# The opening of a hybrid attention and GLA layer: inputs laid out by the host, sums of squares by products with ones, and first groups of one K tile

## The chip, the core and the metric

The kernel runs on one NeuronCore of a Trainium2 chip. TensorE (PE) multiplies matrices from SBUF into PSUM; VectorE (DVE) and ScalarE (ACT) do the elementwise work; GpSimd (POOL) here does little but start transfers; SyncE (SP) starts nearly all the loads of weights. Each engine runs its own list of instructions in the order of the built program and waits on semaphores for the others. The metric is the device time of one execution in microseconds (us): the median of the runs, and, for where the time goes, one profiled execution.

## What is computed

One layer (batch 1, 256 latent tokens, 256 context tokens, width 2048, everything in float32). Only the latent stream is returned. The part that the change touches is the beginning: the modulation and the first columns of the input projection.

```python
def rms_norm(x, g):
    xf = x.astype(jnp.float32)
    y = xf * lax.rsqrt(jnp.mean(xf * xf, axis=-1, keepdims=True) + EPS)
    return (y * g.astype(jnp.float32)).astype(x.dtype)

def modulate(x, g, shift, scale):
    return rms_norm(x, g) * (1 + scale) + shift
...
mod_x = jnp.split((jax.nn.silu(c) @ w_mod[l] + b_mod[l])[:, None, :], 6, axis=-1)
mod_c = jnp.split((jax.nn.silu(c_ctx) @ w_mod[l] + b_mod[l])[None, None, :], 6, axis=-1)
...
qa, ka, va, qb, kb, vb, rb, gf, gb, gate_a, gate_b = proj(modulate(x, g_mix[l], mod_x[0], mod_x[1]))
...
cqa, cka, cva, cqb, ckb, cvb, crb, cgf, cgb, cgate_a, cgate_b = proj(modulate(ctx, g_mix[l], mod_c[0], mod_c[1]))
```

`h @ w_in` is cut into the inputs of two token mixers: windowed attention (qa, ka, va) and gated linear attention, GLA (qb, kb, vb, rb, and a low-rank decay). Their outputs are merged by sigmoid gates and projected; then comes a convolutional feed-forward part with `w_up` and `w_down`.

## The kernel before

The stream h = modulate(x) is kept transposed, with the 2048 channels on partitions in 16 K tiles of 128, and 256 tokens in the free dimension; s = 0 is the latent stream, s = 1 the context. Every float32 operand of the large products is split into a high part (`hi`, rounded to the fast float32 format) and a remainder (`lo`), and a product is three fast products: hi.hi, lo.hi and hi.lo. Weights arrive as `raw` [128, 2, 512] (two K tiles of 512 columns, 512 KB); `wsplit_raw` (lines 223 to 236) makes `whi` on ScalarE (L227) and `wlo` on VectorE (L228). The products themselves all go through `mm` (L83).

**The opening** (lines 114 to 660) needs shift and scale of a K tile before that K tile of h exists. `mod_both` (from line 329) computes both streams' modulation for a group of K tiles: `mraw` loads of 1 MB from `w_mod`, small products with SiLU(c) and SiLU(c_ctx) in `cS` into four quarters of a PSUM bank (`pm`, L95), a transposition on VectorE (`mtr`, L347), a product with `sel` that adds the quarters (`pcol`), four copies and the bias (L357, L360). A group of n K tiles takes n loads for the scale (part 1) and n for the shift (part 0). The groups are `[(0, 2), (2, 2), (4, 4), (8, 4), (12, 4)]` (line 449): first K tile and number.

For each group the kernel computes four blocks of columns of the projection over the group's K tiles and adds them up in SBUF: `qb` (two blocks of 512 columns, latent only), `kbt` (512 columns of K, both streams) and `vb0` (512 columns of V, both streams). That is done in this order so that the first products can start before all of `w_mod` has arrived. `affine_scale` (L528, L531) multiplies by the scale and the row factor, `affine_shift` (L538, L539) adds the shift and splits into hi and lo.

**Tokens before.** x and ctx are loaded as rows of tokens; TensorE transposes them in 128x128 pieces (`turn_tokens`, L481), ScalarE and VectorE copy the pieces into `xr`. The squares are summed per token (`square`, L472, L473), `rms_scale` makes a factor per token on [128, 2], and a product of ones with a diagonal matrix spreads it to a row for all partitions (`factor_row`, L503). The parameters c, b_mod, g_mix and the like are loaded as rows and turned by TensorE (`columns`).

**Order of work.** Inside the opening `pe_seq` chains all of TensorE's instructions in the order of the program text, and `load` chains the loads on SP's queue. VectorE's and ScalarE's lists are ordered by a scheduler at build time; `hold`, `hold_hi` and `in_order` place a few instructions by hand. `idle(n)` puts n transposes of the identity on TensorE. `bg_steps` holds the modulation steps of the next group, which `tick` issues between blocks at `bg_rate`. The tiles named M share 16 buffers of 8 KB per partition (line 37): xr, kbt, vb0, the h tiles, mraw and others; `raw` has 7, `whi` and `wlo` 3 each, the PSUM banks `acc` 4.

After the opening come the low-rank decay products (`plr`, L695, its first consumer of the whole of h), GLA, attention, merge and the feed-forward part. TensorE works through these one after the other.

Of the kernel before, what the change touches and what calls it, by code (L numbers as in the profile page):

```python
# [8 lines left out]
F32 = mybir.dt.float32  # L9
# [7 lines left out]
P = 128  # L17
D = 2048
# [12 lines left out]
def layer_kernel(ctx, tc, A, out):  # L31
# [81 lines left out]

    ident = cst.tile([P, P], F32, name="ident")
    load(ident, A["k_ident"])
    x00 = M("x00", [P, D])
    load(x00, A["x"][0][0:P, :])
    crow = sm.tile([32, P], F32, name="crow", tag="t128", bufs=2)
    nc.scalar.dma_start(crow[0:16, :], A["c"][0].rearrange("(k p) -> k p", p=P))
    nc.scalar.dma_start(crow[16:32, :], A["c_ctx"].rearrange("(k p) -> k p", p=P))  # L120
    sel = cst.tile([P, 34], F32, name="sel")
    G.dma_start(sel, A["k_sel"])
    ones = cst.tile([P, P], F32, name="ones")
    V.memset(ones, 1.0)

    silu_c = S.activation(crow, crow, AF.Silu)
    with tc.issue_after(silu_c.ins):
        S.preload_act_table_set("natural_log_exp_and_others")
    cS = W2("fb", "cS", [P, KT, 32])
    V.memset(cS, 0.0)  # L130
    ccol = cst.tile([P, KT], F32, name="ccol")
    pt = bank("pc0", (P, 32))
    PE.transpose(pt, crow, ident[:32, :32])
    for i in range(2):
        V.tensor_copy(cS[:, :, i], pt[:, 16 * i:16 * i + 16])
    V.tensor_copy(ccol, pt[:, 0:16])

    def columns(name, parts, eng=G, put=None):
        rows = sm.tile([P, P], F32, name="rows", tag="t128", bufs=2)
        n = 0  # L140
        for ap in parts:
            k = ap.shape[0] // P
            eng.dma_start(rows[n:n + k, :], ap.rearrange("(k p) -> k p", p=P))
            n += k
        t = cst.tile([P, n], F32, name=name)

        def turn():
            pt = bank("pt_" + name, (P, P))
            turn_b(pt[:, :n], rows[:n, :], ident[:n, :n])
            V.tensor_copy(t, pt[:, :n])  # L150

        if put is None:
            turn()
        else:
            put(turn)
        return t

    turn_c1 = []
    c1 = columns("c1", [A["b_mod"][0], A["g_mix"][0], A["g_ffn"][0]], put=turn_c1.append)
    bmod, gmix, gffn = c1[:, 0:96], c1[:, 96:112], c1[:, 112:128]  # L160
# [168 lines left out]
    def mod_both(part, t0, n, dst, put=None):  # L329


        a = []
        c0, w = part * D + t0 * P, n * P
        nk = 16 // n

        def step(k0):
            if k0 == 0:
                a.append(bank(f"pm{part}_{t0}", (P, w), side=True))
            raw = M("mraw", [P, nk, w])
            load(raw, w_mod[k0 * P:(k0 + nk) * P, c0:c0 + w].rearrange("(c p) d -> p c d", p=P))  # L340
            for k in range(nk):
                kt = k0 + k
                q = 32 * (kt % 4)
                mm_b(a[0][q:q + 32, :], cS[:, kt, :], raw[:, k, :], start=(kt < 4), stop=(kt >= 12))
            if k0 == KT - nk:
                tr = W2("fb", "mtr", [P, n, 4, 32])
                V.transpose(tr.rearrange("p a b c -> p (a b c)"), a[0])  # L347
                a.append(tr)
                if put is not None:
                    put(end)  # L350

        def end():
            pc = bank(f"pcol{part}_{t0}", (32, n * 4, 2))
# [4 lines left out]
            b0 = part * 16 + t0  # L358
            d = dst[:, :, t0:t0 + n]
            V.tensor_tensor(d, d, bmod[:, b0:b0 + n].unsqueeze(1).to_broadcast([P, 2, n]), op=ALU.add)  # L360

        steps = [lambda k0=k0: step(k0) for k0 in range(0, KT, nk)]
# [71 lines left out]
    def rms_scale(ss, n, shape):  # L434
# [14 lines left out]
    groups = [(0, 2), (2, 2), (4, 4), (8, 4), (12, 4)]  # L449
    mods = [[mod_both(part, t0, n, dst, put) for part, dst in ((1, scale1), (0, shift1))]  # L450
            for (t0, n), put in zip(groups, [None, None] + 3 * [lambda fn: defer(0, fn)])]

    xr = [M(f"xr{i}", [P, 8, T]) for i in range(4)]
# [4 lines left out]
    def load_tokens(s):  # L458
        x = []
        for t in range(2):  # L460
            x_ = x00
            if s or t:
                x_ = M(f"x{s}{t}", [P, D])
                load(x_, A["ctx" if s else "x"][0][t * P:(t + 1) * P, :])
            x.append(x_)
        return x

    def square(eng, x_, t, ss):

        junk = (kbt, vb0)[t].rearrange("p a b -> p (a b)")  # L470
        if eng is S:
            return S.activation(junk, x_, AF.Square, accum_out=ss[:, t:t + 1]).ins  # L472
        return V.scalar_tensor_tensor(junk, x_, 1.0, x_, op0=ALU.mult, op1=ALU.mult,  # L473
                                      accum_out=ss[:, t:t + 1]).ins

    def turn_tokens(s, t, x_):
        for g in range(4):
            pt = bank("ptx", (P, 4, P), side=True)
            for k in range(4):
                kt = g * 4 + k  # L480
                i = PE.transpose(pt[:, k, :], x_[:, kt * P:(kt + 1) * P], ident)  # L481
                if not s + t + kt:
                    opening[:] = [i.ins]
                pe_seq(i)
            dst = xr[2 * s + g // 2][:, (g % 2) * 4:(g % 2) * 4 + 4, t * P:(t + 1) * P]
            if g % 2:
                i = V.tensor_copy(dst, pt).ins
            else:
                S.activation(dst, pt, AF.Copy)
        return i  # L490

    def factors(ss):
        cols = rms_scale(ss, D, [P, 2])
        dgs = [sm.tile([P, P], F32, name="dg", tag="t128", bufs=2) for _ in range(2)]
        for t in range(2):
            V.tensor_scalar(dgs[t], ident, cols[:, t:t + 1], None, op0=ALU.mult)
        return dgs

    def factor_row(s, dgs):

        pr = bank("pr", (P, T), side=True)
        for t in range(2):
            pe_seq(PE.matmul(pr[:, t * P:(t + 1) * P], ones[:, 0:P], dgs[t], start=True, stop=True))  # L503
        r = W2("fa", f"rrow{s}", [P, T])
        S.activation(r, pr, AF.Copy)
        rrow1.append(r)
# [19 lines left out]
    def affine_scale(s, t0, n):  # L526
        sc = scale1[:, s, t0:t0 + n]
        V.scalar_tensor_tensor(sc, sc, 1.0, gmix[:, t0:t0 + n], op0=ALU.add, op1=ALU.mult)  # L528
# [34 lines left out]


    x_t = load_tokens(0)
    sums = [sm.tile([P, 2], F32, name="ss0", tag="ss0", bufs=2) for _ in range(2)]
    square(S, x_t[0], 0, sums[0])
    i = turn_tokens(0, 0, x_t[0])
    in_order(i, square(V, x_t[1], 1, sums[0]))
    turn_tokens(0, 1, x_t[1])  # L570
    turn_c1[0]()
    (a0, a1, ea), (b0, b1, eb) = mods[0]
    a0()
    dgs = factors(sums[0])
    a1()
    factor_row(0, dgs)
    idle(8)
# [3 lines left out]
    idle(12)  # L581
    b1()
    idle(6)
    eb()
    idle(14)
    more_h(0)
    qb0 = [W2("fc", "qb0", [P, 512]) for _ in range(4)]
    kts = ALL[0:2]
    early.extend(wload(w_in[0:2 * P, QB + j * 512:QB + j * 512 + 512]) for j in range(2))
    x_t = load_tokens(1)  # L590
    raws = [wload(w_in[0:2 * P, c:c + 512]) for c in (KB, VB)]
# [3 lines left out]
    proj_T(w_in, QB, kts, [h_all(0)], add_to(lambda i: qb0[i], True))  # L595
    sq0 = square(S, x_t[0], 0, sums[1])
    sq1 = square(V, x_t[1], 1, sums[1])
    proj_T(w_in, QB + 512, kts, [h_all(0)], add_to(lambda i: qb0[2 + i], True))
    in_order(last_lo[0], sq1)
    hold_hi.append(sq0)  # L600
    hold.append(sq1)
    early.append(wsplit_raw(raws[0]))
    dgs = factors(sums[1])
    for t in range(2):
        turn_tokens(1, t, x_t[t])
    early.append(wsplit_raw(raws[1]))
    (a0, a1, ea), (b0, b1, eb) = mods[1]
    a0()
    factor_row(1, dgs)
    a1()  # L610
    affine_scale(1, *groups[0])
    affine_shift(1, *groups[0])

    def mid_k():
        ea()
        b0()
        for s in range(2):
            affine_scale(s, *groups[1])

    def mid_v():  # L620
        eb()
        hi.append(affine_shift(0, *groups[1])[1])

    def evac_v(i, b):
        if i < 2:
            V.tensor_copy(vb0[:, i, :], b)
        else:
            in_order(hi[0], S.activation(vb0[:, i, :], b, AF.Copy).ins)

    hi = []  # L630
    proj_T(w_in, KB, kts, [h_all(0), h_all(1)], add_to(lambda i: kbt[:, i, :], True), mid=mid_k)
    b1()
    early.extend(wload(w_in[2 * P:4 * P, c:c + 512]) for c in (QB, QB + 512, KB, VB))
    proj_nat(w_in, 0, VB, kts, h_xc, evac_v, mid=mid_v)
    affine_shift(1, *groups[1])

    for gi, (t0, n) in enumerate(groups):
        if gi == 0:
            continue
# [5 lines left out]
        if gi + 1 < len(groups):  # L645
            bg_steps.extend(mods[gi + 1][0] + mods[gi + 1][1])
            ticks = 4 * ((n + 1) // 2)
            bg_rate[:] = [(1.4 if gi > 1 else 1.0) * len(bg_steps) / ticks + 0.01, 0.0]
        if t0 == 8:
            more_h(1)  # L650
        for s in range(2):
            if gi > 1:
                affine_scale(s, t0, n)
                affine_shift(s, t0, n)
# [4 lines left out]
        proj_nat(w_in, 0, VB, kts, h_xc, add_to(lambda i: vb0[:, i, :], False), mid=flush if gi == 1 else None)  # L659
# [649 lines left out]
```

## Time and profile before

| | us |
|---|---|
| median of 3 runs | 2007.79 (2007.24 to 2007.80) |
| span of the profiled execution, first to last instruction | 2005.1 |
| first product with `w_in` (L83) | starts 27.87 |
| first decay product (L695), after the opening | starts 209.29 |

The page gives no time of its own for the profiled execution beside its span; the median lies 2.7 us above the span. In a time line each row has the start, the length, the engine, the line, the operation, output and inputs with their shape, the count where several are merged, and in brackets the idle time of the engine before it and what ended that. A float32 product that isn't in the fast format appears as two records for one instruction. A row of waits gives who waited for whom, the total, the number of times and the longest.

### The profile page before, as it was taken

The numbers are of one execution on the slowest core, as the hardware profiler recorded it, in microseconds if no ns is written. First come the engines' busy times: TensorE is split into PE (matmuls) and PEld (weight loads), VectorE is DVE, ScalarE is ACT, GpSimd is POOL, SyncE is SP. The second block draws the span as 40 slices with busy tenths as digits, with TensorE's granted clock in tenths as the row PEclk, the third lists the DMA queues.
The fourth block names the chain that finished last, engine by engine and source line by source line (L and its number), as shares of the span: only waits on it lengthen the run. The fifth ranks groups of instructions, "written<-read, shape, count | busy, mean of one in ns | idle before, by whom it ended". The sixth has DMA issues, their size and how long they took to land.

```text
span 2005.1 us, 27521 instructions
## 1 busy us (share of the span) xinstructions
PE 1977.6 (99%) x10450; PEld 1645.9 (82%) x10450; DVE 1435.7 (72%) x2241; ACT 960.5 (48%) x1395; POOL 45.0 (2%) x66
## 2 busy tenths in 40 slices
PE   7999999999999999999999999999999999999999
PEld 5679888888877777888888888888888888888887
DVE  5666667877858888978876455898887555667754
ACT  4323464562345655444444444655555334555532
POOL 1000010011000000000000000000000000000000
PEclk9999999999999999999999999999999999999999
DMA  9986222326754456888886665587876656666563
GB/s 338 386 295 187 86 84 74 104 78 215 222 171 114 126 173 197 286 287 289 286 283 230 233 208 189 170 292 255 257 240 218 215 191 190 189 189 189 190 213 113
DMA packets 214149, 413.56 MB, mean 206 GB/s; under 512 B 12420, under 2 KB 20884, under 8 KB 212992
## 3 DMA queue, kind: packets, MB, share of 16 engines
q1 hardware_dynamic: 212464, 406.96, 63.4%
q0 software_dynamic: 1488, 4.82, 0.8%
q8 instruction: 82, 1.34, 0.3%
q14 instruction: 51, 0.42, 0.1%
q10 hardware_dynamic: 64, 0.02, 0.0%
HBM read 409.63 MB, written 2.11 MB: 205 GB/s over the span
## 4 chain that ended last, share of the span: by engine, by line
PE 60%; issue 16%; DVE 0%; POOL 0%; ACT 0%; DMA 0%; DVEq 0%; POOLq 0%
PE acc L83 47%; PE accs L83 12%; PE pto L98 0%; POOL att L913 0%; DMA glan<-in_gla_norm 0%; PE ptx L98 0%; POOL att L911 0%; PE pcl L95 0%; DVE yd L1252 0%; DVE yd L1246 0%; ACT yo L1128 0%; ACT whi L227 0%; ACT x1T L1136 0%; DVE og L1059 0%; DVE dg L1169 0%
## 5 line engine op out<-in xcount | busy, mean ns | idle before, releaser
L227 ACT ACTIVATE whi<-raw 128x1024 fp32r<-128x1024 f32 x568 | 601.5, 1059 | 814.6 <-PE acc L83 635.4
L228 DVE TENSOR_TENSOR wlo<-raw,whi 128x1024 fp32r<-128x1024 f32 x568 | 693.8, 1223 | 406.3 <-ACT whi L227 345.8
L391 DVE SCALAR_TENSOR_TENSOR macc<-raw,ccol,macc 128x512 f32<-128x512 f32 x240 | 179.8, 749 | 3.8
L83 PE MATMUL acc<-h,whi 128*128 128x512 f32 x704 | 176.9, 393 | 0.6 <-DVE h L523 0.6
L83 PE MATMUL accs<-h,whi 128*128 128x512 f32 x704 | 176.3, 392 | 0.0
L83 PEld LDWEIGHTS acc<-h,whi 128*128 128x128 f32 x704 | 126.5, 189 | 23.7 <-DVE h L523 0.9
L83 PEld LDWEIGHTS accs<-h,whi 128*128 128x128 f32 x704 | 126.6, 189 | 22.6
L83 PE MATMUL acc<-whi,h00hi 128*128 128x512 f32 x352 | 140.4, 399 | 1.0 <-DVE val L62 0.5
L83 PE MATMUL acc<-whi,h01hi 128*128 128x512 f32 x352 | 140.2, 398 | 0.0
L83 PE MATMUL acc<-whi,h00lo 128*128 128x512 f32 x352 | 138.4, 393 | 0.0
L83 PE MATMUL acc<-whi,h01lo 128*128 128x512 f32 x352 | 138.0, 392 | 0.0
L83 PE MATMUL acc<-whi,al 128*128 128x512 f32 x352 | 137.1, 389 | 0.0
L83 PE MATMUL acc<-whi,ah 128*128 128x512 f32 x352 | 137.0, 389 | 0.0
L83 PEld LDWEIGHTS acc<-h,wlo 128*128 128x128 f32 x704 | 96.2, 190 | 7.0
L83 PEld LDWEIGHTS accs<-h,wlo 128*128 128x128 f32 x704 | 96.0, 190 | 6.9
L83 PE MATMUL acc<-wlo,h01hi 128*128 128x512 f32 x352 | 98.6, 395 | 0.0
L83 PE MATMUL acc<-h,wlo 128*128 128x256 f32 x704 | 98.3, 282 | 0.0
L83 PE MATMUL accs<-h,wlo 128*128 128x256 f32 x704 | 98.2, 282 | 0.0
L83 PE MATMUL acc<-wlo,h00hi 128*128 128x512 f32 x352 | 97.8, 394 | 0.0
L83 PE MATMUL acc<-wlo,ah 128*128 128x512 f32 x352 | 94.5, 389 | 0.0
L83 PEld LDWEIGHTS acc<-whi,h00hi 128*128 128x128 f32 x352 | 66.4, 189 | 16.5 <-DVE val L62 1.0
L83 PEld LDWEIGHTS acc<-whi,ah 128*128 128x128 f32 x352 | 66.1, 188 | 13.6
(393 smaller groups left out, 3473.3 us busy)
## 6 DMA issues: line engine op xcount, KB each, us to landing
raw<-in_w_in SPq DMA_DIRECT2D x208, 512.0 KB, 4.5
raw<-in_w_up SPq DMA_DIRECT2D x176, 512.0 KB, 4.3
raw<-in_w_mod SPq DMA_DIRECT2D x128, 512.0 KB, 4.5
raw<-in_w_down SPq DMA_DIRECT2D x88, 512.0 KB, 3.7
mraw<-in_w_mod SPq DMA_DIRECT2D x32, 1024.0 KB, 13.4
raw<-in_w_attn_o SPq DMA_DIRECT2D x32, 512.0 KB, 4.9
raw<-in_w_gla_o SPq DMA_DIRECT2D x32, 512.0 KB, 5.1
raw<-in_w_out SPq DMA_DIRECT2D x32, 512.0 KB, 3.7
```

Source lines behind the costliest of these rows:

```text
L83: r = pe_seq(PE.matmul(*a, **k))
L227: j = S.activation(hi[:, 0:n, :], raw[:, 0:n, :], AF.Copy).ins
L228: i = V.tensor_tensor(lo[:, 0:n, :], raw[:, 0:n, :], hi[:, 0:n, :].bitcast(F32), op=ALU.subtract).ins
L391: i0 = V.scalar_tensor_tensor(a[0], raw[:, k, :], ccol[:, kt:kt + 1], a[0], op0=ALU.mult, op1=ALU.add).ins
```

## The change

- The host lays out x and ctx transposed by K tiles (`xT`, `ctxT`), c and c_ctx as columns (`k_c`), the parameters as columns (`k_cols1`, `k_cols2`), and the shift and scale columns of `w_mod` by group and load (`w_mod01`), so that a load of 1 MB is 8 KB in a row on each partition.
- The transposes of tokens and parameters, the sums per token and the diagonal matrices go. The latent stream's squares are summed over channels by 16 products with ones into `pr`; the context's squares are added up on VectorE first and take one product. The row factor is then computed on a full [128, 256] row, on all partitions alike. The Newton step's factor -0.5 moves into `gm1`.
- The groups become `[(0, 1), (1, 1), (2, 2), (4, 4), (8, 4), (12, 4)]`. The first two have one K tile each, with one load per modulation part, a plain copy in place of the transposition, and their own loads of weights (`wrow`: one K tile of 1024 columns of qb, or 512 of K beside 512 of V) and products (`row_T`, `row_nat`).
- The order of the first two groups: latent K tile 0; modulation of K tile 1 with its column products; the context's product with ones; latent qb of K tile 1; the context's K and V of K tile 0; modulation of the next group between the K and V products of K tile 1.
- The four column turns of conv_w, conv_b and the gate biases become one load of `cw`. The background rate for the first group of two K tiles is set by hand.

```diff
+    def load_tokens(s):
+        for i in range(4):
+            k = slice((i % 2) * 4, (i % 2) * 4 + 4)
+            load(xr[2 * s + i // 2][:, k, :], A["ctxT" if s else "xT"][i // 2, :, k, :])
...
-    silu_c = S.activation(crow, crow, AF.Silu)
+    silu_c = S.activation(cS[:, :, 0:2], crow, AF.Silu)
...
+    V.tensor_scalar(gm1, gmix, -0.5, None, op0=ALU.mult)
...
-            load(raw, w_mod[k0 * P:(k0 + nk) * P, c0:c0 + w].rearrange("(c p) d -> p c d", p=P))
+            load(raw, A["w_mod01"][part, t0 + i].rearrange("p (c d) -> p c d", c=nk))
...
+                if n == 1:
+                    tr = W2("fb", "mtr", [P, P])
+                    V.tensor_copy(tr, a[0])
...
+            if n == 1:
+                pc = bank(f"pcol{part}_{t0}", (P, 2, 1))
+                mm_b(pc[:, :, 0], a[1], sel[:, 0:2], start=True, stop=True)
+                V.tensor_tensor(d, pc, bias, op=ALU.add)
+                return
...
-    groups = [(0, 2), (2, 2), (4, 4), (8, 4), (12, 4)]
+    groups = [(0, 1), (1, 1), (2, 2), (4, 4), (8, 4), (12, 4)]
...
+    def square_sums(s, dst):
+
+        pr = bank("pr", (P, T), side=True)
+        for i in range(4):
+            x_, o = (t[:, (i % 2) * 4:(i % 2) * 4 + 4, :] for t in (xr[2 * s + i // 2], dst[i // 2]))
+            if i % 2:
+                V.tensor_tensor(o, x_, x_, op=ALU.mult)
             else:
+                S.activation(o, x_, AF.Square)
+            if s == 0:
+                for k in range(4):
+                    pe_seq(PE.matmul(pr, ones[:, 0:P], o[:, k, :], start=(i + k == 0), stop=(i + k == 6)))
+        if s:
+            a, b = dst
+            V.tensor_tensor(a, a, b, op=ALU.add)
+            for n in (4, 2, 1):
+                V.tensor_tensor(a[:, 0:n, :], a[:, 0:n, :], a[:, n:2 * n, :], op=ALU.add)
+        return pr
+
+    def factor_row(pr):
+
+        r = W2("fa", "rrow", [P, T])
+        u = W2("fa", "vrow", [P, 2, T])
+        v, t = u[:, 0, :], u[:, 1, :]
+        V.tensor_scalar(v, pr, 1.0 / D, EPS, op0=ALU.mult, op1=ALU.add)
+        S.activation(r, v, AF.Ln)
+        S.activation(r, r, AF.Exp, scale=-0.5)
+        V.tensor_tensor(t, r, r, op=ALU.mult)
+        V.tensor_tensor(t, t, v, op=ALU.mult)
+        V.scalar_tensor_tensor(r, t, -3.0, r, op0=ALU.add, op1=ALU.mult)
...
+    def wrow(kt, c0, step):
+
+        raw = wr.tile([P, 2, 512], F32, name="raw", tag="raw")
+        load(raw, w_in[kt * P:(kt + 1) * P, c0:c0 + 2 * step].rearrange("p (b c) -> p b c", b=2)[:, :, 0:512])
+        return raw
...
+    opening[:] = [pe_seq(PE.transpose(warm[:, 0:P], ident, ident)).ins]
+    idle(16)
+    pr = square_sums(0, [t.rearrange("p a b -> p (a b)").rearrange("p (a b) -> p a b", a=8) for t in (kbt, vb0)])
+    idle(6)
+    (a0, ea), (b0, eb) = mods[0]
     a0()
+    factor_row(pr)
+    idle(6)
     ea()
     b0()
     affine_scale(0, *groups[0])
+    idle(10)
     more_h(0)
     qb0 = [W2("fc", "qb0", [P, 512]) for _ in range(4)]
+    raws = [wrow(0, QB, 512), wrow(0, KB, 1024)]
+    eb()
+    idle(6)
     i, j = affine_shift(0, *groups[0])
     hold.append(i)
     hold_hi.extend([None, j])
+    wq = wsplit_raw(raws[0])
+    load_tokens(1)
+    wkv = wsplit_raw(raws[1])
+    row_T(0, wq, (0, 1), [h_all(0)], add_to(lambda i: qb0[i], True))
+    row_T(0, wkv, (0,), [h_all(0)],
+          lambda i, b: V.tensor_copy(kbt[:, 2 * i:2 * i + 2, 0:T], b.rearrange("p (f t) -> p f t", f=2)))
+    row_nat(0, wkv, h_x, lambda i, b: S.activation(vb0[:, i, :], b, AF.Copy))
+    (a0, ea), (b0, eb) = mods[1]
     a0()
+    b0()
+    raws = [wrow(1, QB, 512), wrow(1, KB, 1024)]
+    ea()
+    eb()
+    affine_scale(0, *groups[1])
+    i, j = affine_shift(0, *groups[1])
+    hold.append(i)
+    hold_hi.append(j)
+    sq = [M(f"sq{i}", [P, 8, T]) for i in range(2)]
+    pr = square_sums(1, sq)
+    pe_seq(PE.matmul(pr, ones[:, 0:P], sq[0][:, 0, :], start=True, stop=True))
+    wq = wsplit_raw(raws[0])
+    row_T(1, wq, (0, 1), [h_all(0)], add_to(lambda i: qb0[i], False))
+    factor_row(pr)
+    for g in (0, 1):
+        affine_scale(1, *groups[g])
+        affine_shift(1, *groups[g])
+    wkv1 = wsplit_raw(raws[1])
+    row_T(0, wkv, (0,), [h_all(1)],
+          lambda i, b: V.tensor_copy(kbt[:, 2 * i:2 * i + 2, T:2 * T], b.rearrange("p (f t) -> p f t", f=2)))
+    row_nat(0, wkv, [h_tok(1, 0), h_tok(1, 1)], lambda i, b: S.activation(vb0[:, 2 + i, :], b, AF.Copy))
+    for fn in mods[2][0]:
+        fn()
+    row_T(1, wkv1, (0,), [h_all(0), h_all(1)], add_to(lambda i: kbt[:, i, :], False))
+    for fn in mods[2][1]:
+        fn()
     early.extend(wload(w_in[2 * P:4 * P, c:c + 512]) for c in (QB, QB + 512, KB, VB))
+    row_nat(1, wkv1, h_xc, add_to(lambda i: vb0[:, i, :], False))
...
-            bg_rate[:] = [(1.4 if gi > 1 else 1.0) * len(bg_steps) / ticks + 0.01, 0.0]
+            bg_rate[:] = [1.4 * len(bg_steps) / ticks + 0.01, 0.0] if gi > 2 else [1.3, -2.0]
...
+    cw = cst.tile([P, 368], F32, name="cw")
+    G.dma_start(cw, A["k_cols2"])
```

231 lines of the change are left out of this document (75 added, 156 removed).

## The prediction, made before the result was seen

> **What bounds the kernel now.** I read the head of the page first, then the busy time by stage, then the time line of the opening engine by engine, because every edited line but a few belongs to the first 209 us.
>
> ```profile
> span 2005.1 us, 27521 instructions
> PE 1977.6 (99%) x10450; PEld 1645.9 (82%) x10450; DVE 1435.7 (72%) x2241; ACT 960.5 (48%) x1395; POOL 45.0 (2%) x66
> PE 60%; issue 16%; DVE 0%; POOL 0%; ACT 0%; DMA 0%; DVEq 0%; POOLq 0%
> ...
> 14.50:17.50 3.00, 1.07 (x16) 0.50 (x16) 1.96 (x9) 0.41 (x2) 0.00 (x0) 1.00 1.09 349
> 17.50:21.20 3.70, 3.45 (x23) 2.19 (x24) 0.45 (x1) 0.33 (x1) 0.00 (x0) 0.54 1.09 350
> 24.00:27.80 3.80, 3.80 (x42) 2.85 (x40) 1.39 (x7) 1.55 (x3) 0.00 (x0) 1.00 1.05 417
> 34.20:43.40 9.20, 7.65 (x73) 5.08 (x71) 7.03 (x17) 5.93 (x13) 1.05 (x3) 1.00 1.09 348
> 43.40:84.90 41.50, 41.02 (x303) 28.99 (x302) 27.20 (x65) 11.63 (x21) 1.03 (x2) 1.00 1.05 382
> 84.90:209.20 124.30, 123.15 (x877) 103.02 (x873) 77.83 (x136) 39.09 (x52) 7.52 (x12) 1.00 0.75 247
> ```
>
> The window rows give stretch, length, busy time of PE, PEld, DVE, ACT and POOL, granted clock, DMA share and GB/s. TensorE is busy to 99% and is the only engine with a share in the chain of waits, so a microsecond in which TensorE has no product ready is a microsecond of time. In the opening the DMA share is also full (1.05 to 1.09), yet from 43.4 on TensorE is busy in 41.02 of 41.5 us: the feed keeps pace. The median of the runs, 2007.8, is 2.7 us over the span; I sum against the span and add 2.7.
>
> ```profile
> 7.04 3.87 PE L481 MATMUL ptx<-ident,x 128*128 128x128 f32 x16
> 24.35 1.07 PE L95 MATMUL pm<-mraw,cS 128*32 128x256 f32 x16
> 27.87 0.39 PE L83 MATMUL acc<-h00hi,whi 128*128 128x256 f32 x1
> 33.33 1.12 PE L83 MATMUL acc<-h00hi,wlo 128*128 128x256 f32 x8
> 34.29 1.47 PE L481 MATMUL ptx<-ident,x 128*128 128x128 f32 x12
> 40.30 1.07 PE L95 MATMUL pm<-mraw,cS 128*32 128x256 f32 x16 [0.25 <-ACT xr L489]
> 74.76 2.48 DVE L548 TENSOR_TENSOR kb<-kb,acc 128x512 f32<-128x512 f32 x4 [1.78 <-PE acc L83]
> 81.97 1.19 PE L83 MATMUL acc<-wlo,h00hi 128*128 128x512 f32 x4
> 209.29 0.64 PE L695 MATMUL plr<-h00hi,wlr 128*32 128x256 f32 x8
> ```
>
> Products with w_in run without a break from 27.87 to the decay products at 209.29. Eight 128x256 products follow each other in some 0.96 us, 0.12 each; four 128x512 ones in 1.03, 0.26 each. One modulation load (16 records) costs TensorE 1.07. VectorE adds 128x512 from the accumulators in 0.62 (four in 2.48).
>
> **The start.** The change loads x already turned, so x's 32 transposes go, and forms the sum of squares by sixteen full float32 products with ones.
>
> ```profile
> 6.77 1.28 ACT L128 ACT_TABLE_LOAD   x1
> 11.56 2.28 DVE L473 SCALAR_TENSOR_TENSOR vb<-x 128x2048 f32<-128x2048 f32 x1
> 14.97 0.28 DVE L150 COPY c<-pt_c 128x128 f32<-128x128 f32 x1
> 20.87 0.38 ACT L505 ACTIVATE rrow<-pr 128x256 f32<-128x256 f32 x1 [5.07 <-PE pr L503]
> 22.80 0.17 DVE L360 TENSOR_TENSOR scale<-scale,c 128x4 f32<-128x4 f32 x1
> 22.89 1.53 PE L562 MATMUL warm<-ident 128*128 128x128 f32 x12
> 23.00 0.23 DVE L528 SCALAR_TENSOR_TENSOR scale<-scale,c 128x2 f32<-128x2 f32 x2
> 23.29 0.88 DVE L531 SCALAR_TENSOR_TENSOR xr<-xr,scale,rrow 128x256 f32<-128x256 f32 x2
> 25.49 0.45 DVE L347 STREAM_TRANSPOSE mtr<-pm 128x256 f32<-128x256 f32 x1 [1.32 <-PE pm L95]
> 27.31 0.91 ACT L538 ACTIVATE h00hi<-xr,shift 128x256 fp32r<-128x256 f32 x2 [1.15 <-DVE shift L360]
> 269.01 1.03 PE L95 MATMUL pa<-q,kf 128*128 128x256 f32 x4
> 269.88 1.03 PE L95 MATMUL pa<-q,kg 128*128 128x256 f32 x4
> ```
>
> The price of such a product: two (four records) start 0.87 us after the two before, so 0.43 each, sixteen 6.9. Seventeen warm-up transposes at the cold rate (3.87 for 16), from some 4.4 us, when I take the identity to have landed, end at about 8.5; ScalarE's first square is ready by then, since its second table load ends by 8.05 as now. So the sums end near 15.4. Behind them come six small steps on DVE and ACT (0.38 to 0.48 each with hand-over) and the 0.28 copy, 3.0 in all; the scale's bias, factor and first multiplication, 0.9: 19.3. The shift's products, its copy, ten warm-ups, column product and bias run beside that and end at 20.9; hi takes 0.5 and the first product starts near 21.7 instead of 27.87: **-6.2**. Bounds: with the sums at the full clock from the start and loads as early as now, 20.5; with a cold clock for half the sums (8 x 0.43 more), 25.
>
> **Context tokens.** Their 32 transposes and what waits on them fill TensorE from 34.29 to 40.30: **-6.0**. In their place stands one product with ones (0.43), counted in the next wait. Against this, only two modulation loads instead of four lie ahead of the first product, so two more lie behind it, and a load for one K tile needs 32 records of half the width: 2 x 1.07, and between nothing and 0.5 more for each of the two narrow ones behind it (sixteen weight loads take 0.50 in the row from 14.5 to 17.5): **+2.5**.
>
> **What opens in between.** With one K tile, little work is ready. The built program's order on VectorE, which runs it in that order, shows three places where TensorE stands.
>
> First: x's part of K tile 0 is 36 products of 256 and 6 of 512 columns, 5.7 us, to about 27.9; the two loads of K tile 1 last to 30.7. Their column products need two copies of the sums, but VectorE has ahead of the first copy: two evacuations of K (0.62 each), two squares of the context (1.2 each) and the addition of 128x2048 (2.28), which waits for ScalarE's two squares, themselves behind the evacuation of V. That addition ends near 33.3. Then copy, additions of 1024 and 512, second copy, two biases, an addition of 256, factor, multiplication: 3.7; hi and the conversion of the next weights on ScalarE, 1.5 (0.46 and the 1.06 of whi): product at 38.5. From 30.7 that is 7.8, less 0.6 for the three small products in it: **+7.2**. Behind the blocked column product stand all of TensorE's later instructions.
>
> ```profile
> L227 ACT ACTIVATE whi<-raw 128x1024 fp32r<-128x1024 f32 x568 | 601.5, 1059 | 814.6 <-PE acc L83 635.4
> L228 DVE TENSOR_TENSOR wlo<-raw,whi 128x1024 fp32r<-128x1024 f32 x568 | 693.8, 1223 | 406.3 <-ACT whi L227 345.8
> ```
>
> Second: the 24 query products end at 41.4, but the context's factor row stands on VectorE behind two wlo (2.4) and four additions to qb (4 x 0.62): 38.5 + 2.4 + 2.5 = 43.4, then three steps of the factor, a multiplication and hi, 2.3: 45.7. **+4.3**.
>
> Third: in the first group of two K tiles the second lo stands on VectorE behind wlo, the first lo, four additions to vb and two more wlo. From the shift's column product: copies and bias 0.82, 3 x 1.2, 4 x 0.62, two lo 0.9, together 7.8; TensorE has 12 products of 512 and three of 256 columns for it, 3.4. **+4.4**. Twice, too, a column product follows its loads with nothing between them, so it waits out the transposition (0.45 and hand-overs): **+2.0**. At the group of four K tiles five loads and both column products stand together ahead of the first product, and lo waits for copies, factor, four multiplications and one wlo (4.4 against 1.5 of work, and 1.5 for the second column product, less the 0.8 below): **+3.5**.
>
> Now there are waits there as well, which go with the old order:
>
> ```profile
> PEld pm L95 <- DMA mraw<-in_w_mod: 2.1, 3, 1.1
> ...
> PEld acc L83 <- ACT h10hi L538: 1.1, 2, 0.8
> PEld acc L83 <- ACT h00hi L538: 0.8, 1, 0.8
> ...
> PEld acc L83 <- DVE h10lo L539: 0.3, 1, 0.3
> ```
>
> 2.1, 1.1 and 0.3: **-3.5** (the 0.8 is used above). Bounds of the five waits together (21.4): half, if the steps on VectorE overlap better than added up, and a quarter more, 27, if each hand-over costs 0.1.
>
> **The clock.** In 14.5 to 17.5 TensorE was busy for 1.07 of 3.0 us, and in the next 3.7 us the granted clock was 0.54. Waits of 7.2, 4.3 and 4.4 us leave such stretches; each costs half of some 3.5 us, 1.75. Bounds 0 and 5.3 (all three); I take two: **+3.5**. "TensorE: Matmul & The Clock Gate" of the Trainium skill (Part 1) says that a window of about 3.4 us must be idle before the clock is halved. By that rule only the first wait is sure to hold one, and the sum would be 1.75 less, 2017.8; the row shows the fall after a window that was a third busy.
>
> Hidden or nothing: the column turns of conv_w and its like (three or four products of under 0.3) go, a gain under 1. The loads laid out for the host's order change no byte count. Past the opening the engines' orders differ in a few neighbouring steps only, which I cost at nothing.
>
> **Sum.** -6.2 - 6.0 + 2.5 + 7.2 + 4.3 + 4.4 + 2.0 + 3.5 - 3.5 + 3.5 = +11.7. Span 2016.8, time **2019.5**.
>
> **The rivals.** *The feed sets the pace (faster).* If the weights' arrival paced TensorE until the DMA share falls, the waits would cost nothing, and only arrival would count. Rows of 8 KB moved at 417 GB/s (24.0 to 27.8, the context's rows among them), rows of 1 KB at 348 (34.2 to 43.4), of 2 KB at 382. The 8 MB of modulation weights that came in 1 KB rows would arrive 4.0 us sooner, the 24 MB in 2 KB rows 5.6: 9.6 less the 2.5 of work added above, 2001. For it: DMA shares above 1 up to 84.9. Against it: TensorE waited 2.1 us for these weights in all and was busy in 41.02 of 41.5. It decides only if TensorE's waits for weights exceed those for VectorE. "DMA: Bandwidth & Descriptors" of the skill (Specifications) names a limit of 358 GB/s for a core's share of HBM; by it there would be no gain, but the 417 of this trace stands above it.
>
> *The waits are half as long.* VectorE's backlog drains sooner and the clock holds: -6.2 - 6.0 + 2.5 + 10.7 - 3.5 = -2.5 at the least, with 19 of the 21.4 and no clock loss +5.8, that is 2005 to 2014; I take 2011. For it: the waits above add up whole durations, and every overlap of two steps shortens them. Against: VectorE's order is fixed.
>
> *Starved as well.* sq0, sq1 and the eight h tiles hold big buffers, so modulation loads of the four-tile group go out late and TensorE waits some 4 us for them, and the start slips to 25 (+3.3): 2027. For it: that pool has 16 buffers. Against it: four token tiles no longer take buffers of their own, and two MB fewer come ahead of the first product.
>
> **How the numbers follow.** The sum 0.70, with its own range 2013 to 2025 (the bounds of clock, start and waits in part); the half waits 0.12; starved 0.09; the feed 0.09. This kernel's measurement can tell about 0.2% from no change, 4 us: faster is below 2003.8, slower above 2011.8. Faster 0.09 (the feed), same 0.08 (most of the half waits), slower 0.83. The range takes in the half waits and part of starved: 2009 to 2026.
>
> **What would show it.** Right: the first w_in product at 21 to 23 us; TensorE without products for over 6 us near 30 to 38, released by VectorE and ScalarE, and twice for over 4 before 70; a granted clock near 0.5 after one; the first decay product near 221. Wrong: the first product later than 25; waits named for mraw; the context's product with ones done before the loads of K tile 1; the decay products before 212.

## The result, and the profile after

The changed kernel takes 2026.97 us, the median of four runs (2025.95 to 2027.31), beside 2007.51 of the kernel before in the same session: ratio 1.0095, 95% interval 1.0082 to 1.0108. It is slower, by 19.5 us; the forecast was 2019.5, with a range of 2009 to 2026. Its profiled execution took 2027.22 with a span of 2025.5, 20.4 more than the span before.

The head of the page of the changed kernel, with the shares of the chain of waits:

```profile
span 2025.5 us, 27541 instructions
PE 1983.8 (98%) x10479; PEld 1655.3 (82%) x10479; DVE 1443.1 (71%) x2237; ACT 956.6 (47%) x1383; POOL 41.2 (2%) x59
PE 59%; issue 16%; POOL 0%; DVE 0%; ACT 0%; DMA 0%; DVEq 0%; POOLq 0%
```

On the whole page little has moved; the loss lies in one stage that these averages hide. Its end can't be read from the first decay product, as the prediction meant to: before, 24 products of the next block (2.9 us) stood ahead of it, now they come after it. The last product with `wlo` of the opening is the fair mark. It starts at 205.31 before and at 226.32 now, 21.0 later; from there to the end the new kernel loses nothing more (it wins 0.6). The busy time of the engines from the first product with `w_in` to that mark, first before, then after:

```profile
27.87:205.31 177.44, 174.12 (x1267) 139.35 (x1266) 113.25 (x214) 60.77 (x89) 9.05 (x15) 1.00 0.86 294
```

```profile
24.20:226.32 202.12, 181.22 (x1299) 146.64 (x1299) 125.29 (x233) 58.16 (x82) 6.91 (x11) 0.93 0.71 261
```

The stretch is 24.7 longer and starts 3.7 sooner. Of the 24.7, TensorE stood idle for 17.6 (20.9 of its 202.12 now, 3.3 before) and was busy 7.1 longer, although the context's transposes, 6 us with the waits among them, are gone: the granted clock fell from 1.00 to 0.93 and the DMA share from 0.86 to 0.71. The time line of TensorE after shows where:

```profile
6.19 0.48 PE L572 MATMUL warm<-ident 128*128 128x128 f32 x1 [6.19 <-DMA ident<-in_k_ident]
...
9.88 4.79 PE L459 MATMUL pr<-kb,ones 128*128 128x256 f32 x16
14.50 3.62 PE L459 MATMUL pr<-vb,ones 128*128 128x256 f32 x16
...
24.20 0.39 PE L83 MATMUL acc<-h00hi,whi 128*128 128x256 f32 x1
...
36.18 0.59 PE L95 MATMUL pcol<-sel,mtr 128*128 128x2 f32 x2 [3.48 <-DVE mtr L329]
38.31 0.59 PE L95 MATMUL pcol<-sel,mtr 128*128 128x2 f32 x2 [1.54 <-DVE scale L344]
...
41.22 0.58 PE L83 MATMUL acc<-h00hi,whi 128*128 128x256 f32 x1 [1.27 <-ACT whi L209]
...
50.32 0.58 PE L83 MATMUL acc<-h10hi,whi 128*128 128x256 f32 x1 [3.70 <-ACT h10hi L510]
...
58.81 0.23 PE L95 MATMUL pcol<-mtr,sel 128*32 128x16 f32 x2 [0.58 <-DVE mtr L332]
...
64.64 0.24 PE L95 MATMUL pcol<-mtr,sel 128*32 128x16 f32 x2 [0.67 <-DVE mtr L332]
72.41 0.58 PE L83 MATMUL acc<-h00lo,whi 128*128 128x256 f32 x1 [3.78 <-DVE h00lo L511]
100.48 0.19 PE L95 MATMUL pcol<-mtr,sel 128*32 128x32 f32 x1 [1.44 <-DVE scale L350]
102.74 0.39 PE L83 MATMUL acc<-h00hi,whi 128*128 128x256 f32 x1 [1.18 <-ACT h00hi L510]
104.91 0.58 PE L83 MATMUL acc<-h00lo,whi 128*128 128x256 f32 x1 [1.79 <-DVE h00lo L511]
```

Every bracket of these waits names VectorE, or ScalarE that waits for VectorE; none names a load. They stand where the forecast put them. VectorE's own rows around the first and the second show the backlog:

```profile
33.63 2.29 DVE L462 TENSOR_TENSOR sq<-sq,sq 128x2048 f32<-128x2048 f32 x1 [0.85 <-ACT sq L456]
35.84 0.28 DVE L329 COPY mtr<-pm 128x128 f32<-128x128 f32 x1
36.04 1.94 DVE L464 TENSOR_TENSOR sq<-sq 128x1024 f32<-128x1024 f32 x2
37.90 0.28 DVE L329 COPY mtr<-pm 128x128 f32<-128x128 f32 x1
...
45.47 2.48 DVE L520 TENSOR_TENSOR qb<-qb,acc 128x512 f32<-128x512 f32 x4 [1.90 <-PE acc L83]
47.87 0.42 DVE L475 TENSOR_TENSOR vrow<-rrow 128x256 f32<-128x256 f32 x1
```

The sums of K tile 1's modulation are in PSUM by 33, but their copies stand behind the addition of 128x2048 (33.63) and behind two more (36.04). The context's factor, whose part on ScalarE ends at 42.9, waits until 47.87 behind four additions to `qb`, which themselves wait for products (45.47).

Then the clock. These are windows of 3.41 us, laid on the borders at which the granted clock changes in the trace:

```profile
32.71:36.12 3.41, 0.00 (x0) 0.00 (x0) 2.56 (x4) 0.89 (x1) 0.00 (x0) 1.00 1.01 413
36.12:39.53 3.41, 1.81 (x6) 1.43 (x6) 3.02 (x10) 0.00 (x0) 0.00 (x0) 0.50 1.01 399
39.53:42.95 3.42, 2.15 (x10) 1.73 (x9) 2.71 (x5) 3.13 (x5) 0.00 (x0) 0.50 0.99 389
42.95:46.36 3.41, 3.41 (x18) 3.41 (x17) 1.51 (x3) 0.00 (x0) 0.00 (x0) 0.50 1.07 401
46.36:49.78 3.42, 0.26 (x2) 0.06 (x1) 3.32 (x8) 0.02 (x1) 0.00 (x0) 1.00 1.02 423
49.78:53.19 3.41, 2.87 (x12) 2.64 (x13) 1.24 (x4) 0.89 (x2) 0.00 (x0) 0.50 0.34 142
53.19:56.60 3.41, 3.41 (x16) 2.14 (x19) 1.27 (x2) 0.87 (x2) 0.00 (x0) 0.50 0.00 0
...
66.85:70.26 3.41, 1.56 (x8) 0.89 (x6) 3.41 (x6) 2.56 (x4) 0.00 (x0) 1.00 0.85 351
...
97.56:100.98 3.42, 1.98 (x28) 0.65 (x20) 1.62 (x8) 0.26 (x1) 0.00 (x0) 1.00 1.00 407
```

Read each row with the clock of the next one. After windows with 0.00, 0.26 and 1.56 us of work at full clock the next is at half; after 1.98 the next is still full (100.98 to 104.39, granted 1.00), and that one, with 0.96 of work, is followed by half clock again. At half clock, windows with 1.81, 2.15 and 2.87 busy are followed by another half one, those with 3.41 by a full one (so was one with 2.89, from 104.39 on; a border between 2.87 and 2.89 rests on two windows only). So one wait costs one to three windows: half clock begins at a border inside the wait or at its end, and goes on until a window is nearly full of work. Four of the waits make eight such windows, 27.3 us, of which TensorE worked some 21.

### The profile page after: what moved, and what is told of

It is laid out like the page before. It is cut to its first block, busy times and chain, and to the rows that moved or that the text cites. A ratio compares the mean times of both kernels' runs of the same rounds, so it can differ in the third digit from the quotient of the medians.

```text
span 2025.5 us, 27541 instructions
## 1 busy us (share of the span) xinstructions
PE 1983.8 (98%) x10479; PEld 1655.3 (82%) x10479; DVE 1443.1 (71%) x2237; ACT 956.6 (47%) x1383; POOL 41.2 (2%) x59
## 4 chain that ended last, share of the span: by engine, by line
PE 59%; issue 16%; POOL 0%; DVE 0%; ACT 0%; DMA 0%; DVEq 0%; POOLq 0%
PE acc L83 46%; PE accs L83 12%; PE pto L98 0%; POOL att L907 0%; DMA glan<-in_gla_norm 0%; POOL att L905 0%; PE ptx L98 0%; PE pcl L95 0%; DVE yd L1241 0%; DVE yd L1235 0%; ACT yo L1118 0%; ACT whi L209 0%; ACT x1T L1126 0%; DVE og L1053 0%; DVE dg L1159 0%
## 5 line engine op out<-in xcount | busy, mean ns | idle before, releaser
L83 PEld LDWEIGHTS acc<-whi,al 128*128 128x128 f32 x352 | 66.1, 188 | 13.7
```

What stands on the lines that cost most here:

```text
L83: r = pe_seq(PE.matmul(*a, **k))
```

## The experiments

All are kernels of their own, beside the kernel before in their own session (2006.65, 2007.30 and 2006.78 in three sessions). "First" and "last" are the starts of the first and of the last product with `w_in` in the opening, "clock" the granted clock between them. These three are read in the profiled execution, which lay up to 1.5 us from the median of its kernel (warm 2024.11, order4 2022.78, two 2007.94).

| kernel | us | ratio to before (95%) | first | last | clock |
|---|---|---|---|---|---|
| before | 2007.51 | 1 | 27.87 | 205.31 | 1.00 |
| after | 2026.97 | 1.0095 (1.0082 to 1.0108) | 24.20 | 226.32 | 0.93 |
| warm | 2022.65 | 1.0081 (1.0067 to 1.0094) | 22.52 | 222.97 | 0.96 |
| warm2 | 2019.58 | 1.0058 (1.0046 to 1.0071) | 23.84 | 218.11 | 1.00 |
| two | 2006.78 | 1.0002 (0.9993 to 1.0010) | 26.26 | 206.59 | 0.99 |
| order3 | 2021.86 | 1.0077 (1.0063 to 1.0091) | 22.67 | 219.96 | 0.96 |
| order4 | 2023.96 | 1.0083 (1.0069 to 1.0097) | 22.70 | 221.95 | 0.94 |
| ctxsum | 2024.36 | 1.0091 (1.0077 to 1.0105) | 22.29 | 222.78 | 0.96 |
| fast | 2018.60 | 1.0055 (1.0043 to 1.0068) | 20.12 | 217.52 | 0.96 |
| fast_warm | 2012.99 | 1.0030 (1.0018 to 1.0041) | 20.75 | 212.12 | 1.00 |
| ident | 2026.78 | 1.0101 (1.0087 to 1.0115) | 23.89 | 225.88 | 0.93 |
| two_fast | 2001.88 | 0.9975 (0.9966 to 0.9984) | 25.45 | 200.02 | 1.00 |

**The clock by itself: warm and warm2.** Only transposes into banks that are overwritten later are added.

```diff
+    pr = bank("pr", (P, T), side=True)
     a0()
     b0()
     raws = [wrow(1, QB, 512), wrow(1, KB, 1024)]
+    idle(13, pr)
     ea()
+    idle(6, pr)
     eb()
...
+        idle(pre, banks[0])
```

> Edit: transposes of the identity stand in TensorE's waits (13, 6 and 4 around K tile 1's column products, 13 ahead of the context's first product, 13 ahead of the first group of two K tiles, 6 ahead of that of four), into banks that are overwritten later; nothing else moves, VectorE's and ScalarE's steps stay in their order. Theory (the clock): the waits stay as long as they are, but the granted clock stays near 1.0 where it was 0.5 between 36 and 77 us, so that the products there take 2.6 + 3.1 + 2.3 = 8.0 us less; the transposes may overrun by up to 1 us: 2019 to 2021, first decay product at 219 to 221. Rival (the half clock costs nothing, since the products there wait for weights and evacuations anyway): within 1 us of 2027.

The time line of TensorE in warm, at the first of these waits:

```profile
31.17 1.64 PE L534 MATMUL pr<-ident 128*128 128x128 f32 x13
34.49 0.38 PE L95 MATMUL pcol<-sel,mtr 128*128 128x2 f32 x2 [1.68 <-DVE mtr L330]
```

It fell short of the expected 2019 to 2021, and its last product came 3.4 sooner than after's, of which 1.7 is an earlier start. Thirteen transposes took 1.64 us, half of the wait, and the windows behind still went to half clock (0.50 from 38 to 42). So warm doesn't test the theory; warm2 does.

> Edit: as in warm, but with 30, 14 and 6 transposes around K tile 1's column products, 33 ahead of the context's first product, 33 and 12 ahead of the first groups of two and of four K tiles, since a batch of 13 took only 1.64 us there and left 1.7, 1.4, 2.5 and 2.5 us of each wait empty. Theory A (the half clock costs its full 8 to 9.5 us): no half clock left between 30 and 110, 2017 to 2019.5. Theory B (the clock shares its time with VectorE's backlog: products that run faster only wait longer for it): 2021 to 2023, as warm gave, with the waits for VectorE longer by what the products save.

The stretch of warm2, by windows, then its second wait on TensorE's time line:

```profile
23.84:218.11 194.27, 186.80 (x1427) 152.44 (x1427) 125.19 (x233) 57.74 (x82) 6.89 (x11) 1.00 0.75 272
```

```profile
43.74 3.82 PE L534 MATMUL acc<-ident 128*128 128x128 f32 x33
47.84 0.38 PE L83 MATMUL acc<-h10hi,whi 128*128 128x256 f32 x1 [0.28 <-ACT h10hi L510]
```

No half clock is left, and the 0.28 in the bracket shows that the transposes do not overrun there: ScalarE's `h10hi`, which waits for VectorE, still ends the wait. From first to last product it takes 194.27 instead of 202.12: the half clock cost 7.85 us. The time, 7.4 under after's, lies 0.1 above theory A's range (2017 to 2019.5); theory B's 2021 to 2023 is out. That 27.3 us at half clock cost no more has a reason in the rows above: for 6 of them TensorE had nothing to do, and the steps on VectorE for which it waited went on meanwhile.

"TensorE: Matmul & The Clock Gate" of the Trainium skill reckons the loss as the throttled time by the share of the clock withheld (Terms), here 27.3 x 0.5 = 13.7 as an estimate; the runs show 7.85. Its one idle window (Part 1) is not what these rows show either: 1.56 us of work in the window were too little.

**The groups or the layouts: two.** The groups of before with all the rest of the change; the context's squares take sixteen products with ones where its transposes stood.

```diff
-    groups = [(0, 1), (1, 1), (2, 2), (4, 4), (8, 4), (12, 4)]
+    groups = [(0, 2), (2, 2), (4, 4), (8, 4), (12, 4)]
...
+    proj_T(w_in, QB, kts, [h_all(0)], add_to(lambda i: qb0[i], True))
+    proj_T(w_in, QB + 512, kts, [h_all(0)], add_to(lambda i: qb0[2 + i], True))
+    (a0, a1, ea), (b0, b1, eb) = mods[1]
+    sq = [M(f"sq{i}", [P, 8, T]) for i in range(2)]
+    pr = square_sums(1, sq)
```

> Edit: all of the host's layouts and the sums by products with ones stay, but the groups are those of before, (0, 2), (2, 2), (4, 4) and on, in the order of before; the context's squares go through sixteen products with ones where its transposes stood. Theory (the loss is the order of the groups of one K tile, its waits and what they do to the clock): two more modulation loads ahead of the first product bring it to 26 to 28, the context's 6.0 us of transposes become 6.9 of products, the waits and the half clock go: decay product at 206 to 210, time 2003 to 2009. Rival (the layouts or the products with ones themselves cost the time): over 2015. Rival (8 KB rows pace the kernel): under 2000.

TensorE's time line of two:

```profile
26.26 0.38 PE L83 MATMUL acc<-h00hi,whi 128*128 128x256 f32 x1 [0.68 <-ACT h00hi L505]
...
32.67 7.07 PE L459 MATMUL pr<-sq,ones 128*128 128x256 f32 x32
...
43.80 0.38 PE L83 MATMUL acc<-h10hi,whi 128*128 128x256 f32 x1 [1.76 <-ACT h10hi L505]
```

2006.78, no difference from before that can be told. Everything that the change loses, it loses by the groups of one K tile and their order, with the place of the context's sums (ctxsum, below, moves these alone and is 2.6 lower, most of it by an earlier start). The layouts and the sums by products with ones, taken together, neither win nor lose: 1.6 us of earlier start, 7.07 of products in the place of 6.0 of transposes, a wait of 1.76, and one window of half clock.

**VectorE's order: order3 and order4.**

```diff
-            V.tensor_tensor(a, a, b, op=ALU.add)
+            in_order(scaled, V.tensor_tensor(a, a, b, op=ALU.add).ins)
...
-    factor_row(pr)
+    in_order(factor_row(pr), *qadds)
...
+            if s == 0 and gi == 2:
+                in_order(i, vadds[2])
```

> Edit: three orders by hand on VectorE and no other change: K tile 1's sums, biases and multiplication ahead of the addition of 128x2048; the context's row factor ahead of the four additions to qb; the second lo of the first group of two K tiles ahead of vb's last addition. Theory (VectorE's backlog makes the waits): first query product of K tile 1 near 37 instead of 41.2, the context's first product near 46 instead of 50.3, the third wait 1 to 2 shorter: 5 to 7 us less, and one window of half clock fewer (1.7) is possible: 2018 to 2022. Rival (the steps wait for their data, the context's tokens or ScalarE, and the order on VectorE is not what counts): within 1.5 us of 2027.

TensorE's time line of order3:

```profile
40.34 1.22 PE L613 MATMUL pr<-sq,ones 128*128 128x256 f32 x2 [7.83 <-DVE sq L464]
...
45.96 0.35 PE L83 MATMUL acc<-h10hi,whi 128*128 128x256 f32 x1 [0.57 <-DVE qb L617]
48.06 0.39 PE L83 MATMUL acc<-h10lo,whi 128*128 128x256 f32 x1 [1.74 <-DVE h10lo L513]
```

The time is inside its range, and the last product comes 6.4 sooner than after's (1.5 of it by the start). So the order does count (its three places were changed at once, and no run takes them apart), but not where it was expected: the column products are no longer late, and TensorE now waits 7.83 for the product with ones, which stands ahead of the query products in its list. Order4 puts it behind them.

```diff
-    pe_seq(PE.matmul(pr, ones[:, 0:P], sq[0][:, 0, :], start=True, stop=True))
     wq = wsplit_raw(raws[0])
     row_T(1, wq, (0, 1), [h_all(0)], add_q)
+    pe_seq(PE.matmul(pr, ones[:, 0:P], sq[0][:, 0, :], start=True, stop=True))
```

> Edit: order3, and the context's one product with ones goes behind the 24 query products of K tile 1 on TensorE, since in order3 it waited 7.8 us for the last addition of squares with the query products, ready by 37, behind it. Theory (TensorE's own order passed the wait on): the query products start at 36 to 37 and end by 40; the context's first product comes 1 to 3 sooner than in order3 (46.0, with its lo at 48.1): 2018 to 2021. Rival (the context's chain on VectorE, additions, factor, multiplication, sets the end whatever TensorE does before it): within 1 us of order3, 2021 to 2023.

Order4 on TensorE, then on VectorE:

```profile
34.67 0.58 PE L83 MATMUL acc<-h00hi,whi 128*128 128x256 f32 x1 [2.13 <-ACT whi L209]
...
47.29 0.58 PE L83 MATMUL acc<-h10hi,whi 128*128 128x256 f32 x1 [6.11 <-ACT h10hi L512]
```

```profile
43.83 2.47 DVE L616 TENSOR_TENSOR qb<-qb,acc 128x512 f32<-128x512 f32 x4
46.22 0.87 DVE L504 SCALAR_TENSOR_TENSOR xr<-xr,scale,rrow 128x256 f32<-128x256 f32 x2
```

The query products start early, at 34.67, and nothing is won: the context's first product comes at 47.29, 1.3 later than in order3, after a wait of 6.11, and the clock is lower. The time, 2.1 above order3's, lies outside both ranges. In both runs the additions of squares and the factor's steps last until about 44 (43.9 here, 44.3 in order3), whatever TensorE does before; but here the builder put the four additions to `qb` ahead of the multiplication, where order3 has them behind it. With order3's 1.65 from the factor's end to the product (44.31 to 45.96) it would have come near 45.6, an estimate: 0.4 sooner than in order3, where 1 to 3 were expected. The theory falls. VectorE's chain for the context is the bound, and a product moved forward only moves the hole.

**The context's sums on TensorE: ctxsum.**

```diff
-            if s == 0:
+            if True:
...
     raws = [wrow(1, QB, 512), wrow(1, KB, 1024)]
+    sq = [M(f"sq{i}", [P, 8, T]) for i in range(2)]
+    pr = square_sums(1, sq)
     ea()
     eb()
...
-    pe_seq(PE.matmul(pr, ones[:, 0:P], sq[0][:, 0, :], start=True, stop=True))
```

> Edit: the context's squares are summed by sixteen products with ones on TensorE, placed between K tile 1's modulation products and its column products, in place of VectorE's four additions and the one product. Theory (an idle TensorE is what costs, by its wait and by the clock): the sixteen products take 6.9 us at full clock in a wait that was 8.5; the first query product comes at 40 to 41, about as before, but at full clock (2.6 less), and the context's factor is early, so that the second wait falls from 3.7 to 1 to 2 and the context's products run at full clock (3.1 less): 2019 to 2022. Rival (clock without effect): 2024 to 2027. Rival (sixteen more products are simply 6.4 us more work): 2030 to 2034.

2024.36, above the theory's range by 2.4, and within the rival's that the clock has no effect, which warm2 excludes. The last product comes 3.5 sooner than after's, 1.9 of it by the start. TensorE's first wait is filled, and the query products run at full clock from 41.06, but only after a wait of 2.13 for their weights; the second wait is still 2.79 and puts the context's products at half clock, and the third stays at 3.77 with its two windows. The wait filled early took 0.9 off the second and nothing off the third.

**The start: ident.**

```diff
-    nc.scalar.dma_start(crow, A["k_c"])
     ident = cst.tile([P, P], F32, name="ident")
     nc.scalar.dma_start(ident, A["k_ident"])
+    nc.scalar.dma_start(crow, A["k_c"])
```

> Edit: the identity is fetched ahead of the conditioning vectors on ScalarE's queue instead of behind them; no other change. Theory (the start is TensorE's own work from the identity's landing on, with nothing between): the identity lands 0.4 to 1.5 sooner than 5.8 to 6.2, the warm-ups begin that much earlier and the first product with w_in comes as much sooner, at 21 to 23.5: 0 to 2 us off the time, which lies inside the spread that the start of the full clock gives (22.3 to 24.2 so far). Rival (the products with ones wait for the squares, which the tokens' arrival sets): first product where it was, sums begin no earlier than 9.1.

Its start on TensorE's time line:

```profile
5.29 0.47 PE L572 MATMUL warm<-ident 128*128 128x128 f32 x1 [5.29 <-DMA ident<-in_k_ident]
...
10.63 3.72 PE L459 MATMUL pr<-kb,ones 128*128 128x256 f32 x16 [1.77 <-ACT kb L456]
```

The first product stays about where it was (0.3 sooner), as the rival said, but the rival's reason, the tokens' arrival, isn't what the trace shows. The identity came 0.9 sooner than after's, and the sums then waited 1.77 for ScalarE's first square. ScalarE's rows, first in after and then in ident, show why it was late:

```profile
4.55 1.28 ACT L136 ACT_TABLE_LOAD   x1 [4.55 <-DMA crow<-in_k_c]
...
7.38 1.06 ACT L456 ACTIVATE kb<-xr 128x1024 f32<-128x1024 f32 x1
```

```profile
6.68 1.28 ACT L136 ACT_TABLE_LOAD   x1 [6.68 <-DMA crow<-in_k_c]
...
9.52 1.06 ACT L456 ACTIVATE kb<-xr 128x1024 f32<-128x1024 f32 x1
```

The conditioning vectors, now fetched second, landed 2.1 later, and SiLU and the first square behind it came 2.1 later with them. So the edit delayed the squares by itself. What an earlier identity would bring without that, no run shows.

**Cheaper sums: two_fast, fast and fast_warm.** Two_fast is two, and fast is ctxsum, with squares rounded to the fast format, so that each product with ones is one pass; the latent squares also move from `kbt` and `vb0` to tiles of their own. Fast_warm adds to fast the third line of order3 and transposes as in warm.

```diff
+    ones_r = W2("mod", "ones_r", [P, P], F32R)
+    V.tensor_copy(ones_r, ones)
...
-                    pe_seq(PE.matmul(pr, ones[:, 0:P], o[:, k, :],
+                    pe_seq(PE.matmul(pr, ones_r, o[:, k, :],
...
-    sq = [M(f"sq{i}", [P, 8, T]) for i in range(2)]
+    sq = [M(f"sq{i}", [P, 8, T], F32R) for i in range(2)]
```

> Edit: two, with squares and ones in the fast float32 format, so that the sixteen products with ones of each stream are one pass (0.12 us) instead of 0.43. The squares are rounded to that format, which leaves their low parts out of the sums. Theory (these products stand on the path): the first product comes at 22 to 25 instead of 26.3, then the modulation loads are the limit; the context's sums take 2 instead of 6.9, of which the wait for its h10hi (1.8) takes 1 to 3 back: 2000 to 2004. Rival (VectorE's factor steps or the loads take the place): 2005 to 2007.

Two_fast beats both kernels: 2001.88, 0.9975 of before (0.9966 to 0.9984). Its first product, at 25.45, is later than the 22 to 25 expected and only 0.8 sooner than in two; most of the gain lies behind it. The view of TensorE's waits between 20 and 130 has a new first row, who waited for whom, total, times, longest:

```profile
PE pm L95 <- DMA mraw<-in_w_mod: 3.2, 3, 1.4
```

Only with the sums cheap does the feed begin to bound the opening, in the kernel whose other waits in that view are 0.7 and 0.3.

> Edit: ctxsum, the groups of one K tile, with the same fast sums of rounded squares as in two_fast. Theory: the start falls by 3 to 4 (first product at 18 to 19.5), since only two modulation loads lie ahead of it; the context's sums no longer fill the first wait, whose end VectorE's squares and column steps set; 2017 to 2021. Rival (the waits for VectorE come from the groups themselves and grow by what the start gains): 2022 to 2025. In either case it stays well above two and two_fast.

Fast lands inside its range, though its first product, at 20.12, is later than the 18 to 19.5 expected: it is 2.2 sooner than in ctxsum, its last 5.3 sooner. The waits of ctxsum stay (2.13, 2.79, 3.78), and so does the half clock; two waits for `mraw` join them (0.26 and 1.43).

> Edit: fast, with the second lo of the first group of two K tiles ahead of vb's third addition, and transposes of the identity in the waits: 18 ahead of K tile 1's query products, 24 ahead of the context's first product, 28 and 14 ahead of the first groups of two and of four K tiles. Theory (waits and half clock are two costs that add up): fast had products at half clock for some 12 us, 6 us lost; they come back, and 0.6 of the third wait: 2011.5 to 2014, all of it at a clock of 1.0; what stays over two_fast (10 us or more) are the waits of the groups of one K tile by themselves, 2.1, 2.8 and 3.2 in the rows of fast, and 5 in those ahead of the group of four. Rival (faster products only lengthen the waits): 2016 to 2018.

The two costs add up as expected: at a clock of 1.00, with the stretch 6.0 shorter than fast's (191.37 against 197.40). It stays 11.1 above two_fast, and that is the price of one-K-tile groups that the changes in it, fast sums, a full clock and the third of order3's orders, do not take away. The second of those orders was not tried on top of it, and order3 and warm2 were not joined. Bigger changes, such as another place for the context's first products, were not tried.

## Why the prediction was wrong in size and right in kind

Its sign, places and releasers hold. Of the signs that it named, the idle TensorE of over 6 us between products (3.48 + 1.54 + 1.27) and the half clock came. The first product (24.20, not 21 to 23), two waits of over 4 before 70 (3.70, and 3.78 at 72) and the decay product (227.32, not near 221) missed. By the fair mark the opening is 21.0 later, where the sum said 11.7; the 9.3 are made up so:

- **The clock, "+3.5", is the step that failed most.** It took one window at half clock for each of three waits, charged two, and named 5.3 as the bound. The trace has eight windows, behind four waits, and warm2 shows 7.85: 4.4 more than forecast and outside the bound. The row it read, one window at 0.54 after a stretch a third busy, stood before work that then ran full; it says when half clock begins, not how long it lasts while waits follow each other.
- **"-3.5" for the old waits was hardly there.** 2.1, 1.1 and 0.3 are rows of the weight load (PEld). TensorE's matmuls went on during most of them: for `mraw` PE's own row has 0.2 where PEld's has 2.1. The view of PE before, over its opening, has

```profile
PE acc L83 <- DVE wlo L228: 0.9, 2, 0.6
...
PE acc L83 <- DVE h00lo L539: 0.3, 1, 0.3
...
PE pm L95 <- DMA mraw<-in_w_mod: 0.2, 1, 0.2
```

  and no row for `h10hi` or `h10lo`. The waits for `wlo` are there after, too (0.64 and 0.23, at 161.61 and 166.21), and those for `xr` belong to the transposes' 6.0. What could go was 0.5, 3.0 less than the term.
- **The start, "-6.2", gave -3.7.** The identity landed at 6.19 instead of the 4.4 taken, so the products with ones began at 9.88 instead of 8.5, and the sixteen took 8.1 instead of 6.9, the first eight of them 4.62. The granted clock reads 1.00 from 8 to 18 all the same; why the first eight were slower stays open. The start also varies from one kernel to the next with that: 22.3 to 24.2 with the same instructions ahead of it.
- **The five waits, "+21.4", gave about 20.3.** First 7.9 (TensorE free at 32.7, product at 41.22, less the same 0.6) where 7.2 was said, second 3.7 (4.3), third 3.8 (4.4), the column products 0.58 + 0.67 (2.0), the group of four 1.44 + 1.18 + 1.79, less 0.8 (3.5). The steps added up on VectorE were the right ones; "half as long" fell.
- The four add up to 4.4 + 3.0 + 2.5 - 1.1 = 8.8; no run takes the remaining 0.5 apart. The sentence that products with `w_in` run without a break from 27.87 is loose: the transposes that the sum takes off stand between them, at 34.29.

The feed rival fell for this kernel: no wait of TensorE in the opening names `mraw`. The rates it used held (414 GB/s from 11 to 34.8, 373 before), but the bytes came sooner to a TensorE that was waiting for VectorE. "Starved as well" named nearly the right time, 2027, for the wrong reason: its start (25) came near, its wait for loads never came. What lies past the opening cost nothing, as was said.

## What to carry to other kernels

Cutting the first group smaller wins time only if the elementwise steps between groups shrink with it; the earlier first product (3.7 us here) is lost again in the waits behind it. Here TensorE's work per group halved and VectorE's chain did not: its busy time between the first and the last product rose from 113.25 to 125.29. Price a wait of TensorE together with the windows of half clock that it starts, and look whether the next wait comes before one full window has passed. Read waits of the weight load only where the matmul's own row shows them too.

## What the runs showed of the hardware that was not expected

Half clock outlasts its cause: with a hole of 3.48 + 1.54 + 1.27 us it held for three windows, 10.2 us, and a window with 2.87 of 3.41 us busy at half clock was still followed by one at half. It can be prevented by work that does nothing (33 transposes in 3.82 us in the second wait, 128 in all), and that alone was worth 7.4 us of the time. With modulation rows of 8 KB among the loads, the windows above show 389 to 423 GB/s where the DMA share was full. Before, with rows of 1 and 2 KB, it was 348 and 382 (34.2 to 43.4 and 43.4 to 84.9), and 417 where the context's rows of 8 KB were among them (24.0 to 27.8). No run varies the length of the rows alone.
